# A transformer block's down projection in block products joined to the feed-forward, and the low parts of early weights made by other engines

## The chip, the cores and the metric

The kernel runs on one core of one Trainium2 chip. The metric is device time in microseconds, from launch to end. Engines are called PE (TensorE), DVE (VectorE), ACT (ScalarE), POOL (GpSimd) and SP (SyncE), as in the profile. The program has one launch; nothing is computed on the host apart from laying the inputs out.

## The reference, cut

One block on x of 512 tokens by 1024 channels, float32. All weights are float32.

```
h = rms_norm(x, norm1_pre)
q, k, v, z, xbc, dt, gates = split(h @ w_in)          # 512, 128, 128, 1024, 1536, 32, 2048 columns
attn = gqa_attention(rope(rms_norm(q)), rope(rms_norm(k)), v) @ w_attn_proj     # 8 query, 2 key heads of 64
ssd  = ssd_branch(z, silu(conv5(xbc)), dt, ...) @ w_ssd_proj                    # Mamba-2, both directions
g_attn, g_ssd = split(sigmoid(gates))
x  = x + rms_norm((g_attn * attn + g_ssd * ssd) @ w_out, norm1_post)
h2 = rms_norm(x, norm2_pre)
gate, up = split(h2 @ w_gate_up)                       # 2 x 2816 columns
x  = x + rms_norm((silu(gate) * up) @ w_down, norm2_post)                       # w_down: 2816 x 1024
```

## The kernel before

Every large product is made in a rounded float32 form (fp32r): each operand is split into a high part (a cast, on ACT) and a low part (operand minus high part), and a product is three matmuls, low x high, high x low and high x high. A weight tile is 128 rows by 1024 columns (512 KB). Its low part is made in one of three ways, chosen by a letter in `weights` and read in `wnext`/`presplit`: "v", a subtraction on DVE; "g", a subtraction on POOL; "d", ACT writes the negated weight, rounded to fp32r, into the low part's tile (`A.mul(l, raw, -1.0)`), and an accumulating transfer that POOL issues (`G.dma_start(l, src, accum_op=ALU.add)`) adds the weight from memory, which leaves what the rounding dropped. High and low parts have four buffers each, raw tiles three.

The stages, in order of time in the trace: q projection with the first norm (to 33 us); k/v projection, 8 k-tiles with 12 matmuls each (to 47); `xbc`, the x/B/C projection, 12 weight tiles of 24 matmuls, with convolution, rotary embedding and head norms of q and k woven in (to 131); the z projection woven with attention (to 225); gates woven with the state-space part (to about 375); their projections and the mixing (to 446); `out_proj`; the feed-forward's gate and up projection, 22 tiles of hidden channels (about 492 to 728); the down projection, 22 k-tiles (725 to 846); the last norm and the stores.

In `xbc` the order on PE, ACT, DVE and POOL is the written one (`manual_schedule`), by a table `inner` of what stands in the middle and at the end of each tile: `kt(h)` are the transposes of half of the rotated keys (`k_transposed`, two banks "sb", each read by two copies into `kT`), `xt` those of x. In the feed-forward PE's order is the written one and a scheduler places the other engines' instructions, in which `issue_after` sets a bound. Elsewhere the scheduler decides.

The feed-forward multiplies its first three tiles plainly (`NPLAIN`, `prepare_plain`, `plainly`) and the other 19 by seven block products in place of eight (two halves of tokens, two of channels, gate and up), which need sums R1 to R4 of quarters of h2T; `combine` makes these sums for tokens 256 on, and `blocks2` and `blocks3` bring h2T's last tokens (`hilo`: ACT's high, DVE's low part). `row_rstd` makes a diagonal matrix of the row scales, which PE spreads over the partitions (`spread`). `activate` makes the activation tiles `act`, 22 of 128 hidden channels by 512 tokens.

`down` multiplies plainly: for each k-tile the four groups of 128 tokens by two halves of 512 columns, three matmuls each, 24 matmuls of 512 columns, into eight banks; the last four k-tiles are run token group by token group (`token_major8` with `ntail` 4), so that the epilogue of a group (square sum on ACT, gains and residual on DVE, store) runs beside the matmuls of the next.

## Time and profile before

| | us |
|---|---|
| three runs | 847.55, 851.00, 851.08 (median 851.0) |
| profiled execution | 855.7 |
| its span, first to last instruction | 853.8 |
| PE busy | 822.2 (96%) |
| DVE, ACT, POOL busy | 550.2, 434.2, 178.7 |
| mean granted clock of TensorE | 0.986 of 2.4 GHz |

PE is the engine with the most work, so a step costs time where PE waits for it, where it adds matmuls, or where it stands behind the last matmul. A wait has a second effect in this trace, that the granted clock is lower for some microseconds behind it; the windows show it.

### The profile page before, as it was taken

What the parts mean: (1) busy time and instruction counts of PE and PEld (TensorE: products, weight loads), DVE (VectorE), ACT (ScalarE), POOL (GpSimd) and SP (SyncE); (2) the same over time, 40 slices, a digit from 0 to 9 for tenths busy, and PEclk for the clock granted to TensorE, in tenths of its full rate; (3) what the DMA queues carried; (4) which work ended last, traced back from release to release, by engine and by line L of the source; (5) the groups of instructions that cost most, each with busy time, mean ns of one, the idle gap of its engine ahead of it and who ended that gap; (6) DMA issues with size and microseconds to landing.
All of it is one profiled execution on the core that took longest, in us unless ns stands there. A gap on an engine that the chain in (4) does not pass through costs nothing.

```text
span 853.8 us, 12071 instructions
## 1 busy us (share of the span) xinstructions
PE 822.2 (96%) x4570; PEld 689.6 (81%) x4570; DVE 550.2 (64%) x918; ACT 434.2 (51%) x775; POOL 178.7 (21%) x142
## 2 busy tenths in 40 slices
PE   8989899899899999999999989999999999999996
PEld 7768787666666777767888788999999999888885
DVE  3958884965325545676683796788788788533326
ACT  6656585554664434157333655555555556322222
POOL 3323122310113334539551011000000100000000
PEclk9989999999999999999999999999999999999999
DMA  9586551110676665137335542677666674522314
GB/s 309 173 210 146 118 142 51 50 50 0 149 175 145 162 147 137 62 111 221 124 124 196 174 124 72 183 190 196 187 186 175 174 182 151 182 94 95 99 50 148
DMA packets 42826, 120.88 MB, mean 142 GB/s; under 512 B 5264, under 2 KB 5648, under 8 KB 42768
## 3 DMA queue, kind: packets, MB, share of 16 engines
q1 hardware_dynamic: 36000, 95.46, 32.7%
q0 software_dynamic: 6768, 24.64, 16.9%
q8 instruction: 36, 0.59, 0.3%
q14 instruction: 22, 0.18, 0.1%
HBM read 111.70 MB, written 8.39 MB: 141 GB/s over the span
## 4 chain that ended last, share of the span: by engine, by line
PE 78%; DVE 9%; DMA 4%; issue 4%; ACT 3%; POOL 2%; SPq 0%; DVEq 0%; POOLq 0%; ACTq 0%
PE sa L973 10%; PE mm L177 8%; PE mm L178 8%; PE mm L179 8%; PE sc L973 6%; PE mm L973 3%; PE sb L973 3%; PE sc L177 3%; PE sc L179 3%; PE sc L178 3%; PE sa L178 2%; PE sa L179 2%; PE sa L177 2%; PE sc L678 2%; PE sb L177 2%
## 5 line engine op out<-in xcount | busy, mean ns | idle before, releaser
L142 ACT CAST whi<-raw 128x1024 fp32r<-128x1024 f32 (+3 forms) x85 | 85.0, 1003 | 56.1 <-PE sc L179 49.3
L147 POOL TENSOR_TENSOR wlo<-raw,whi 128x1024 fp32r<-128x1024 f32 (+3 forms) x31 | 65.1, 2105 | 93.5 <-ACT whi L142 91.3
L177 PE MATMUL mm<-hT,wlo 128*128 128x512 f32 x176 | 74.7, 425 | 6.5 <-DMA wlo<-in_w_xbc 4.1
L179 PE MATMUL mm<-hT,whi 128*128 128x512 f32 x176 | 70.3, 400 | 0.0
L178 PE MATMUL mm<-hT,whi 128*128 128x512 f32 x176 | 69.9, 397 | 0.0
L147 DVE TENSOR_TENSOR wlo<-raw,whi 128x1024 fp32r<-128x1024 f32 (+1 forms) x26 | 31.7, 1218 | 53.3 <-ACT whi L142 53.3
L1016 POOL DMA_DIRECT2D raw<-in_w_gu x19 | 16.4, 864 | 219.0 <-DVE wlo L1022 60.6
L1021 ACT CAST whi<-raw 128x512 fp32r<-128x512 f32 (+1 forms) x57 | 41.6, 762 | 36.3 <-PE mm L973 15.5
L1022 DVE TENSOR_TENSOR wlo<-raw,whi 128x512 fp32r<-128x512 f32 (+1 forms) x57 | 47.7, 866 | 18.5 <-ACT whi L1021 18.4
L973 PE MATMUL sa<-R,whi 128*128 128x256 f32 x304 | 56.4, 283 | 0.0
L177 PEld LDWEIGHTS mm<-hT,wlo 128*128 128x128 f32 x176 | 33.8, 192 | 17.0 <-ACT wlo L144 4.7
L973 PEld LDWEIGHTS sa<-R,whi 128*128 128x128 f32 x304 | 47.4, 192 | 0.0
L973 PE MATMUL sa<-R,wlo 128*128 128x256 f32 x152 | 43.0, 283 | 0.0
L144 ACT ACTIVATE wlo<-raw 128x1024 fp32r<-128x1024 f32 x28 | 29.7, 1060 | 25.2 <-PE mm L177 24.3
L178 PEld LDWEIGHTS mm<-hT,whi 128*128 128x128 f32 x176 | 33.8, 192 | 8.9 <-issue 2.4
L179 PEld LDWEIGHTS mm<-hT,whi 128*128 128x128 f32 x176 | 33.7, 192 | 7.8 <-issue 0.5
L145 POOL DMA_DIRECT2D wlo<-in_w_g x16 | 14.0, 872 | 108.2 <-ACT wlo L144 58.4
L639 DVE TENSOR_REDUCE nmax<-sa 128x1 f32<-128x512 f32 x32 | 21.6, 686 | 16.2 <-PE sa L637 15.9
L973 PE MATMUL sa<-h2T,b 128*128 128x256 f32 x228 | 30.5, 283 | 0.0
L1124 DVE TENSOR_TENSOR acl<-act,ach 128x512 fp32r<-128x512 f32 x22 | 14.9, 688 | 23.3 <-ACT ach L1123 23.3
L973 PEld LDWEIGHTS sa<-R,wlo 128*128 128x128 f32 x152 | 29.2, 192 | 0.1
L973 PEld LDWEIGHTS sa<-h2T,b 128*128 128x128 f32 x228 | 28.7, 192 | 0.0
(439 smaller groups left out, 2476.5 us busy)
## 6 DMA issues: line engine op xcount, KB each, us to landing
raw<-in_w_gu SPq DMA_DIRECT2D x44, 512.0 KB, 4.6
raw<-in_w_dn SPq DMA_DIRECT2D x22, 512.0 KB, 3.5
raw<-in_w_gu POOLq DMA_DIRECT2D x19, 512.0 KB, 5.3
raw<-in_w_g SPq DMA_DIRECT2D x16, 512.0 KB, 6.0
wlo<-in_w_g POOLq DMA_DIRECT2D x16, 512.0 KB, 6.7
raw<-in_w_xbc SPq DMA_DIRECT2D x12, 512.0 KB, 4.2
wlo<-in_w_xbc POOLq DMA_DIRECT2D x12, 512.0 KB, 8.0
b<-in_w_gu SPq DMA_DIRECT2D x19, 256.0 KB, 5.5
```

The lines of the kernel that those rows point to most:

```text
L142: self.A.copy(h[:, :n], raw[:, :n])
L144: self.A.mul(l[:, :n], raw[:, :n], -1.0)
L147: e.tensor_tensor(l[:, :n], raw[:, :n], h[:, :n].bitcast(F32), ALU.subtract)
L177: self.T.matmul(o, ll, rh, start=first, stop=False)
L178: self.T.matmul(o, lh, rl, start=False, stop=False)
L179: self.last_mm = self.T.matmul(o, lh, rh, start=False, stop=last)
L639: V.tensor_reduce(nmax, ps, AX.X, ALU.max, negate=True)
L678: self.T.matmul(po[i * HD : i * HD + HD, :], self.vt[:, k, g * HD : g * HD + HD], pts[h - 1 + i][k], start=k == 0, stop=k == NT - 1)
L973: self.T.matmul(dst, x, y[:, k], start=start and k == 0 and i == 0, stop=k == 3 and i == 2, skip_group_check=True)
L1016: G.dma_start(p13, wgu[:, 1:3], accum_op=ALU.add)
L1021: A.copy(dst[0], src)
L1022: lo.tensor_tensor(dst[1], src, dst[0].bitcast(F32), ALU.subtract)
```

## The change

Down projection. The first 6 of the 22 k-tiles stay plain, the first two of these in `down_start`, in which the feed-forward's last open product (`late`, returned by `ffn` as a function) is run behind the first bank. The other 16 k-tiles are taken as two halves of 8 (k), two halves of tokens and two of columns, by seven products of blocks in place of eight. Each product has four stages (`product`, `NG2`): a stage splits one weight pair (`wsplit`, 2 x 512 columns) and two operands (`asplit`, 256 tokens) and multiplies with 12 matmuls of 512 columns; the splits stand one stage ahead of the matmuls in the written order, and the scheduler moves them further ahead as buffers allow. Sums of weight blocks are made in place by accumulating transfers (`chain`, `p3`), sums of activations on DVE (`sums`), sums of results in `sums2`, `second`, `sums6`, `sums3` and `last`. The seventh product runs by token group: 6 matmuls in each stage for group 2, then 24 for group 3. `begin` and `finish` are the two halves of the last norm. Per k-tile the plain form has 24 matmuls, so 16 have 384; the seven products have 7 x 48 = 336.

Elsewhere: the letters of `weights`; one broadcast product in place of four in `row_rstd`; q's head-norm product on POOL; all kT copies on ACT; `kt(1)` half a tile later; `combine` behind the last h2T low part; the third plain tile's weights split by 1024 columns; other pools for some tiles.

```diff
         for k0, kn in ((0, 3), (3, 3), (6, 2)):
-            yield a["w_kv"][:, k0 : k0 + kn, :], kn * 288, "v" if k0 == 0 else "g"
+            yield a["w_kv"][:, k0 : k0 + kn, :], kn * 288, "v" if k0 == 0 else "d"
         for j in range(12):
-            yield a["w_xbc"][j], 1024, "d"
+            yield a["w_xbc"][j], 1024, "g" if j < 3 else "d"
         for n in range(2):
             for i in range(4):
-                yield a["w_z"][n, i], 1024, "g"
+                yield a["w_z"][n, i], 1024, "gd"[n]
...
-        for t in range(NT):
-            V.tensor_scalar(diag[:, t], self.ident, dst[:, t : t + 1], None, ALU.mult)
+        V.tensor_tensor(diag, self.ident.unsqueeze(1).to_broadcast([P, NT, P]), dst.unsqueeze(2).to_broadcast([P, NT, P]), ALU.mult)
...
-        self.V.tensor_tensor(lo, src, hi.bitcast(F32), ALU.subtract)
+        self.last_lo = self.V.tensor_tensor(lo, src, hi.bitcast(F32), ALU.subtract)
...
-        r = self.head_norm(*bb, NQ, self.hr[:, 8 * t : 8 * t + 8])
+        r = self.head_norm(*bb, NQ, self.hr[:, 8 * t : 8 * t + 8], self.G)
...
-                (A.copy if g else V.tensor_copy)(dst, p4[:, :, g])
+                self.A.copy(dst, p4[:, :, g])
...
-        inner = {5: ([], [kt(0)]), 6: ([kt(1)], [xt(0, 0)]), 7: ([xt(0, 1)], [xt(0, 2)]), 8: ([xt(0, 3)], []),
+        inner = {5: ([], [kt(0)]), 6: ([xt(0, 0)], [kt(1)]), 7: ([xt(0, 1)], [xt(0, 2)]), 8: ([xt(0, 3)], []),
...
+            if wide:
+                for i, names in enumerate((("B11", "B12"), ("B22", "B21"))):
+                    hl = [self.wp.tile([P, 1024], F32R, tag=s, name=self.nm(s), bufs=4) for s in ("whi", "wlo")]
+                    A.copy(hl[0], raw[i])
+                    V.tensor_tensor(hl[1], raw[i], hl[0].bitcast(F32), ALU.subtract)
...
-        for t in (2, 3):
-            combine(t)
+        with self.tc.issue_after(self.last_lo.ins):
+            for t in (2, 3):
+                combine(t)
...
-                    w = prepare_plain(j)
+                    w = prepare_plain(j, True)
...
+    def down_start(self, late):
+        self.wseq = ((self.a["w_dn"][j], 1024, "v") for j in range(NF - 2 * PAIRS))
+        self.bank, self.ops = {}, []
+        for k in range(2):
+            self.down_operands(k)
+        for tag, n, ts in (("sc", 0, (2, 3)), ("sb", 0, (0, 1)), ("mm", 1, (0, 1)), ("sa", 1, (2, 3))):
+            for t in ts:
+                self.bank[t, n] = self.ps(tag)
+                for k in range(2):
+                    self.plain(k, t, n)
+                if late:
+                    late = late()
...
+            def prep(g):
+                w = wsplit(b(g))
+                for i in range(2):
+                    kept.append((asplit(a(2 * g + i)), [y[:, i * 512 : i * 512 + 512] for y in w]))
+                if after:
+                    G.dma_start(chain[g], after(g), accum_op=ALU.add)
...
+        def sums6():
+            for t in range(2):
+                c[2 + t, 0] = cs.pop()
+                A.copy(c[2 + t, 0], u[t])
+                add(2 + t, 1, u[t], ALU.subtract)
+                add(t, 1, u[t], ALU.subtract)
+                add(2 + t, 0, x[t])
+                begin(2 + t)
...
+        product(u, lambda g: chain[g], a11, True, lambda g: blk(g, 0, 1),
+                lambda k: V.tensor_tensor(r1[k], a22(k), a21(k), ALU.subtract), then=third_weights)
+        product(v, lambda g: raw(g, 1, 0), a12, False, None, lambda k: V.tensor_tensor(a21(k), a11(k), a21(k), ALU.subtract),
+                then=sums2)
+        product(a, lambda g: chain[g], lambda k: r1[k], True, lambda g: blk(g, 1, 1),
+                lambda k: V.scalar_tensor_tensor(r1[k], r1[k], -1.0, a11(k), ALU.mult, ALU.subtract), then=lambda: second(a))
+        product(x, lambda g: p3[g], a21, True, None,
+                lambda k: V.scalar_tensor_tensor(a12(k), r1[k], -1.0, a12(k), ALU.mult, ALU.subtract), then=lambda: second(x))
+        product(u, lambda g: chain[g], lambda k: r1[k], False, lambda g: blk(g, 1, 0), then=sums6)
+        product(a, lambda g: raw(g, 1, 1), a12, False, then=sums3)
+        product(y, lambda g: chain[g], a22, False, None, lambda k: between.get(k, int)(), lambda: last(2))
+        stages[0][0]()
+        for i, (_, work) in enumerate(stages):
+            if i + 1 < len(stages):
+                stages[i + 1][0]()
+            work()
+        last(3)
```

POOL at the start of the program, from the k/v weights to the fourth x/B/C tile. `wlo` is a weight's low part, `raw` the weight, `whi` its high part; "DMA" is the accumulating transfer. Before:

```order
L147 TENSOR_TENSOR wlo_367<-raw_137,whi_366 128x864
L147 TENSOR_TENSOR wlo_379<-raw_139,whi_378 128x576
L145 DMA wlo_440<-in_w_xbc 128x1024
L145 DMA wlo_447<-in_w_xbc 128x1024
L145 DMA wlo_579<-in_w_xbc 128x1024
L145 DMA wlo_586<-in_w_xbc 128x1024
```

and after:

```order
L147 DMA wlo_364<-in_w_kv 128x864
L147 DMA wlo_377<-in_w_kv 128x576
L149 TENSOR_TENSOR wlo_439<-raw_436,whi_438 128x1024
L149 TENSOR_TENSOR wlo_445<-raw_442,whi_444 128x1024
L149 TENSOR_TENSOR wlo_576<-raw_573,whi_575 128x1024
L147 DMA wlo_582<-in_w_xbc 128x1024
```

The two k/v subtractions and the first three x/B/C transfers have changed places in kind; the fourth tile stays a transfer.

DVE at the start of the feed-forward, between the two parts of h2T's last tokens. `h2T` is the low part of a token group, `R` and `af` are the sums of `combine`, `rv`, `rn`, `ry`, `rt` the steps of the row scale, `diag` the diagonal. Before:

```order
L930 TENSOR_TENSOR R_1073_4535<-af_4174,mm_4419 128x512
L161 TENSOR_SCALAR rv_4517<-rv_4517 128x4
L189 TENSOR_SCALAR rn_4520<-rv_4517 128x4
L932 TENSOR_TENSOR R_1075_4537<-mm_4420,R_1074_4536 128x512
L192 RECIPROCAL ry_4521<-rt_4522 128x4
L933 SCALAR_TENSOR_TENSOR R_1074_4536<-R_1075_4537,af_4174 128x512
L206 TENSOR_TENSOR rt_4522<-ry_4521 128x4
L935 SCALAR_TENSOR_TENSOR af_4176<-R_1074_4536,af_4176 128x512
L207 TENSOR_TENSOR rt_4522<-rt_4522,rn_4520 128x4
L208 SCALAR_TENSOR_TENSOR ry_4521<-rt_4522,ry_4521 128x4
L162 COPY rstd_142<-ry_4521 128x4
L183 TENSOR_TENSOR h2T_3918<-sc_4503,h2T_3916 128x4x128
```

and after:

```order
L208 TENSOR_TENSOR rt_4527<-rt_4527,rn_4525 128x4
L209 SCALAR_TENSOR_TENSOR ry_4526<-rt_4527,ry_4526 128x4
L164 COPY rstd_142<-ry_4526 128x4
L166 TENSOR_TENSOR diag_4535<-cst_100,rstd_142 128x512
L184 TENSOR_TENSOR h2T_3918<-sc_4508,h2T_3916 128x4x128
L184 TENSOR_TENSOR h2T_3919<-sc_4509,h2T_3917 128x4x128
L929 TENSOR_TENSOR R_1078_4537<-af_4174,mm_4424 128x512
L994 TENSOR_TENSOR wlo_4684<-raw_4679,whi_4683 128x1024
L931 TENSOR_TENSOR R_1080_4539<-mm_4425,R_1079_4538 128x512
```

The sums stand behind both low parts now, the diagonal ahead of them, and the first wide low part of the third plain tile among the sums.

DVE at the end of the program. `ss`, `rv`, `rn`, `ry` and `rt` are steps of a token group's row scale, `gn` the gain, `x` the residual, `o` (before) and `c` (after) the result, a bank (`mm`, `sc`) holds the last products. Before:

```order
L218 TENSOR_SCALAR ss_8130<-ss_8130 128x1
L1136 TENSOR_TENSOR o_8128<-sc_7309,gn_7299 128x512
L220 TENSOR_SCALAR rv_8136<-ss_8130 128x1
L1136 TENSOR_TENSOR o_8129<-sc_7310,gn_7301 128x512
L189 TENSOR_SCALAR rn_8138<-rv_8136 128x1
L192 RECIPROCAL ry_8139<-rt_8140 128x1
L204 TENSOR_SCALAR rt_8140<-ry_8139,rn_8138 128x1
L208 SCALAR_TENSOR_TENSOR ry_8139<-rt_8140,ry_8139 128x1
L1134 TENSOR_TENSOR ry_8139<-ry_8139,rstd_142 128x1
L1138 SCALAR_TENSOR_TENSOR o_8128<-o_8128,ry_8139,x_1629_8124 128x512
L1138 SCALAR_TENSOR_TENSOR o_8129<-o_8129,ry_8139,x_1630_8125 128x512
```

and after, where four token groups (c_7410 to c_7405 and their second halves) end near each other:

```order
L1264 TENSOR_TENSOR c_7406<-c_7406,gn_7413 128x512
L1270 SCALAR_TENSOR_TENSOR c_7410<-c_7410,ry_8262,x_1693_8233 128x512
L1270 SCALAR_TENSOR_TENSOR c_7408<-c_7408,ry_8262,x_1692_8232 128x512
L1270 SCALAR_TENSOR_TENSOR c_7409<-c_7409,ry_8283,x_1697_8245 128x512
L1270 SCALAR_TENSOR_TENSOR c_7407<-c_7407,ry_8283,x_1696_8244 128x512
L1266 TENSOR_SCALAR rv_8299<-ss_8073 128x1
L1245 TENSOR_TENSOR c_7405<-c_7405,sc_7326 128x512
L190 TENSOR_SCALAR rn_8301<-rv_8299 128x1
L193 RECIPROCAL ry_8302<-rt_8303 128x1
L205 TENSOR_SCALAR rt_8303<-ry_8302,rn_8301 128x1
L209 SCALAR_TENSOR_TENSOR ry_8302<-rt_8303,ry_8302 128x1
L1268 TENSOR_TENSOR ry_8302<-ry_8302,rstd_142 128x1
```

The addition of the last bank (`c_7405<-c_7405,sc_7326`) stands behind the final products of the first two groups.

## Rows read from the trace of the kernel before

**Rows 1.** Page, part 1: busy us, share of the span, instructions of each engine.

```profile
PE 822.2 (96%) x4570; PEld 689.6 (81%) x4570; DVE 550.2 (64%) x918; ACT 434.2 (51%) x775; POOL 178.7 (21%) x142
```

**Rows 2.** Waits of PE: line, what for, us in total, times, longest.

```profile
PE mm L177 <- DMA wlo<-in_w_xbc: 4.1, 2, 3.6
PE sb L654 <- ACT pt L656: 3.2, 1, 3.2
PE sb L372 <- ACT kT L447: 2.7, 1, 2.7
...
PE sa L178 <- DVE h2T L183: 1.9, 1, 1.9
PE sa L177 <- DVE pl L994: 1.5, 1, 1.5
...
PE sa L286 <- DVE diag L165: 1.3, 1, 1.3
```

**Rows 3.** Windows: stretch, length, busy PE, PEld, DVE, ACT, POOL, clock, DMA share, GB/s.

```profile
57.00:63.00 6.00, 6.00 (x16) 4.59 (x16) 4.81 (x14) 0.00 (x0) 2.98 (x5) 0.53 1.06 279
93.00:99.00 6.00, 5.99 (x27) 5.03 (x28) 4.86 (x8) 3.98 (x7) 0.88 (x1) 0.72 0.19 44
165.00:175.00 10.00, 6.91 (x25) 3.02 (x26) 4.48 (x8) 2.86 (x5) 4.42 (x2) 0.83 0.45 157
510.00:514.00 4.00, 4.00 (x24) 4.00 (x23) 3.92 (x7) 1.73 (x3) 1.20 (x1) 0.59 0.00 0
733.24:744.12 10.88, 10.88 (x50) 9.01 (x48) 3.79 (x5) 3.15 (x4) 0.00 (x0) 1.00 0.56 192
```

**Rows 4.** Timeline at 28 to 57: start, us, instruction, idle before; POOL, then PE.

```profile
29.32 4.46 POOL L147 TENSOR_TENSOR wlo<-raw,whi 128x864 fp32r<-128x864 f32 x2 [3.60 <-ACT whi L142]
...
47.36 0.87 POOL L145 DMA_DIRECT2D wlo<-in_w_xbc  x1 [6.86 <-ACT wlo L144]
...
38.78 0.29 PE L178 MATMUL sb<-wlo,hT 128*128 128x288 f32 x1
...
56.56 0.76 PE L177 MATMUL mm<-hT,wlo 128*128 128x512 f32 x1 [3.59 <-DMA wlo<-in_w_xbc]
```

**Rows 5.** Timeline at 30, DVE.

```profile
29.94 4.38 DVE L183 TENSOR_TENSOR hT<-h,hT 128x512 fp32r<-128x512 f32 x2
```

**Rows 6.** The tile wlo at 36 to 80: its transfers.

```profile
DMA to landing us min/median/max: 7.7/9.1/11.8
```

**Rows 7.** Timeline at 92, DVE, then ACT.

```profile
92.13 0.75 DVE L447 CAST kT<-sb 128x256 fp32r<-128x256 f32 x2
...
92.58 0.70 ACT L447 CAST kT<-sb 128x256 fp32r<-128x256 f32 x2 [5.56 <-DVE kT L447]
```

**Rows 8.** Timeline at 162, POOL, then DVE.

```profile
162.13 4.95 POOL L147 TENSOR_TENSOR wlo<-raw,whi 128x1024 fp32r<-128x1024 f32 x2 [26.04 <-ACT whi L142]
...
162.43 2.48 DVE L515 CAST stl<-ones 128x128 fp32r<-128x128 f32 x1
```

**Rows 9.** Timeline at 505 to 509, ACT, then DVE.

```profile
505.84 0.59 ACT L182 CAST h2T<-sc 128x512 fp32r<-128x512 f32 x1
...
507.56 1.28 DVE L183 TENSOR_TENSOR h2T<-sc,h2T 128x512 fp32r<-128x512 f32 x2
```

**Rows 10.** Groups by form: count | busy us, mean ns | idle before and its releasers.

```profile
L147 DVE TENSOR_TENSOR wlo<-raw,whi 128x1024 fp32r<-128x1024 f32 x25 | 30.6, 1225 | 53.3 <-ACT whi L142 53.3
...
L1022 DVE TENSOR_TENSOR wlo<-raw,whi 128x1024 fp32r<-128x1024 f32 x19 | 23.2, 1220 | 4.8 <-ACT whi L1021 4.8
...
L1021 ACT CAST whi<-raw 128x1024 fp32r<-128x1024 f32 x19 | 19.9, 1049 | 18.1 <-DMA raw<-in_w_gu 15.2 <-PE sa L973 2.9
...
L1099 DVE TENSOR_TENSOR g<-g,sa 128x256 f32<-128x256 f32 x19 | 7.9, 416 | 1.6 <-PE sa L973 1.1 <-ACT g L1098 0.5
```

**Rows 11.** Timeline of the tail from 846, ACT, then DVE.

```profile
846.62 0.69 ACT L153 ACTIVATE junk<-sc,rstd 128x512 bf16<-128x512 f32 x1 [1.94 <-PE sc L179]
...
849.11 1.41 DVE L1138 SCALAR_TENSOR_TENSOR o<-o,ry,x 128x512 f32<-128x512 f32 x2
```

More of the change, by code (lines that the diff above doesn't have):

```diff
@@ L42 @@
 R_DTB, R_AL, R_D, R_QK, R_END = 0, 32, 64, 80, 336
+PAIRS = 8
 NPLAIN = 3
@@ L1038, in ffn @@
         rb = late = None
+        spare = [self.cp.tile([P, S], F32, tag=tag, name=self.nm("act")) for tag in ("lT", "rT", "vt")]
+        spare += [self.tp.tile([P, S], F32, tag="spill", name=self.nm("act"), bufs=2) for _ in range(2)]
         def activate(j, up, sign, g):
@@ L1109, in ffn @@
             late = (j, w, u, x7, pw, g)
-        finish(*late)
-    def down(self):
-        V, A = self.V, self.A
-        g = self.gain("norm2_post", "e")
-        self.wseq = ((self.a["w_dn"][j], 1024, "v") for j in range(NF))
-        split = {}
-        def lhs(k):
-            for i in range(k // 2 * 2, min(k // 2 * 2 + 4, NF), 2):
-                if i not in split:
-                    split[i] = hi, lo = [self.sp.tile([P, 2, S], F32R, tag="R", name=self.nm(n), bufs=8) for n in ("ach", "acl")]
-                    for e in range(2):
-                        A.copy(hi[:, e], self.act[i + e])
-                        V.tensor_tensor(lo[:, e], self.act[i + e], hi[:, e].bitcast(F32), ALU.subtract)
-            return [h[:, k % 2] for h in split[k // 2 * 2]]
-        def epilogue(t, po):
-            x = [self.slot("e", [512], name="x2") for _ in range(2)]
+        return lambda: finish(*late)
@@ new lines, in mm3f, with plain, down_operands @@
+    def mm3f(self, o, a, b, start=False):
+        for i, (x, y) in enumerate(((a[1], b[0]), (a[0], b[1]), (a[0], b[0]))):
+            self.T.matmul(o, x, y, start=start and i == 0, stop=i == 2, skip_group_check=True)
+    def plain(self, k, t, n):
+        ah, al, (wh, wl) = self.ops[k]
+        tok, c = slice(t * P, t * P + P), slice(n * 512, n * 512 + 512)
+        self.mm3f(self.bank[t, n], (ah[:, tok], al[:, tok]), (wh[:, c], wl[:, c]), k == 0)
+    def down_operands(self, k, pool=None):
+        ah, al = (pool.tile([P, S], F32R, tag="pa", name=self.nm("pa"), bufs=6) if pool else self.slot("a", [S], F32R, "pa")
+                  for _ in range(2))
+        self.hilo(ah, al, self.act[k])
+        self.ops.append((ah, al, self.wnext()))
@@ new lines, in down, with third_weights, sums2 @@
+        u = [self.ps("sa") for _ in range(2)]
+        a = [self.ps("mm") for _ in range(2)]
+        x = [self.ps("sb") for _ in range(2)]
+        v, y = [bank[t, 0] for t in (0, 1)], [bank[t, 0] for t in (2, 3)]
+        def third_weights():
+            for g in range(NG2):
+                self.load(p3[g], blk(g, 0, 1))
+                G.dma_start(p3[g], blk(g, 1, 1), accum_op=ALU.add)
+        def sums2():
+            for t in range(2):
+                c[t, 0] = cs.pop()
+                A.copy(c[t, 0], v[t])
+                add(t, 0, u[t])
@@ new lines, in second, with sums3 @@
+        def second(p):
+            for t in range(2):
+                add(2 + t, 1, p[t], ALU.subtract)
+        def sums6():
+            for t in range(2):
+                c[2 + t, 0] = cs.pop()
[4 more added lines that the diff above has]
+                begin(2 + t)
+        def sums3():
+            for t in range(2):
+                add(t, 1, a[t], ALU.subtract)
```

138 lines of the change are left out of this document (112 added, 26 removed).

## The prediction

> **What bounds the kernel now.** I read the busy line of the page first: TensorE is busy 822.2 us of a span of 853.8 [rows 1], so 31.6 us are idle and the rest is matmuls. Then the waits of PE by cause [rows 2], to see at which places the idle time lies. Then the granted clock in windows behind each of these waits [rows 3], because a wait here is followed by matmuls at the lower of the two levels (1.2 instead of 2.4 GHz; a figure of 0.5 is the lower one): a stretch of T us at a mean clock of c loses T x (1 - c). Last the other engines' timelines at these places [rows 4 to 9], to see what ended late and why. The down projection shows no wait of PE at all: 48 matmuls in 10.88 us at a clock of 1.00 [rows 3], 0.2267 us each. It is bound by the number of matmuls; DVE works 3.79 and ACT 3.15 us of that window.
>
> The sum is made against the profiled execution, 855.7 us with a span of 853.8. It lies 4.7 above the median of 851.0, which I take off at the end.
>
> **Part 1, low parts of the early weights.** (a) x/B/C: PE waits for the low part of tile j = 1 3.6 us (4.1 with the 0.5 for j = 0) [rows 2]. POOL issues that transfer at 47.36 [rows 4]; such transfers took 7.7 to 11.8 us to land there [rows 6]. Behind the wait the clock is 0.53 over 6 us [rows 3], a loss of 6 x 0.47 = 2.8. In all 6.9 us. The change lets POOL subtract for j = 0, 1 and 2: 4.95 us for two of that size [rows 8], so 2.4 to 2.5 each; even if the operand of j = 1 were ready only when POOL issued before (47.4), the low part stands at 49.9, against a need at 53.0 (the matmul at 56.56 less its wait [rows 4]) less the 1 us that PE comes earlier. The wait has no successor that I can see for j = 1 and 2. For j = 3, the first by transfer, the buffer and cast are there some 10.9 us (two tiles of 24 matmuls) before PE wants it, against a landing of 9.1 in the middle and 11.8 at most: 0 to 1 us of wait. I take **-6.5** (bounds -3.5 and -6.9).
>
> The price of POOL's subtractions is paid by DVE. The rows show it: a DVE copy of 128 columns took 2.48 us beside POOL's pair at 162 [rows 8], the two h low parts 4.38 us beside POOL at 29.3 [rows 5, 4], against 1.28 for two of the same size at 507.56 [rows 9]. The Trainium skill (SBUF — State Buffer, section "SBUF: two separate sides") states that GpSimd and VectorE, when VectorE has two SBUF inputs, lock a shared port pair for a whole instruction, so that the later of the two stands still; the trace agrees with its 2.48 and 4.38, and by this rule each added instruction of POOL can stop one of DVE's for its whole length, which would make the time that of R2 below. At 47 to 57 it is a transfer that PE waits for and not DVE, so the sum has nothing for this, and R2 has its price.
>
> (b) k/v: the low parts of groups 2 and 3 go from POOL to transfers. DVE's h low parts then need 1.3 instead of 4.38 us [rows 5], and the diagonal, for which PE waits 1.3 [rows 2], is one instruction of 512 columns (0.64 by the pair in 1.28 [rows 9]) instead of four. Against it: ACT's cast of group 2 is done at 29.3, when POOL starts [rows 4]; in the new order two h casts (0.59 each [rows 9]) and a negation (0.9 of the 1.05 for 1024 columns [rows 10]) follow before the transfer, so it is issued at about 31.4 and lands between 39.1 and 43.2 by the 7.7 to 11.8 [rows 6], while k-tile 3 came at 38.6 [rows 4] and would now come 1 us earlier. From 2.5 gained to 3 lost; I take **-1.0**, next to the 7.7: an estimate, since the bytes of other transfers that are under way there are not known.
>
> (c) z, second half: from POOL to transfers. PE waits 3.2 us for attention's transposed probabilities [rows 2], and the clock is 0.83 over 165 to 175 [rows 3], of which PE works about 7 us: 1.2 lost. POOL's pair (4.95) held up a DVE copy on that path for 2.48 [rows 8]. That goes; but ACT gets four negations of 1.05 [rows 10] in a stage in which it also writes the probabilities. Bounds 0 and -4.4; I take **-2.5**.
>
> **Part 2, kT copies and the second kT transpose.** PE waits 2.7 us [rows 2] for a bank that is read by two kT copies of DVE at 92.13, which stand behind DVE's other work; ACT's copies follow DVE's, and ACT had been idle 5.56 us [rows 7]. The clock behind it is 0.72 over 6 us [rows 3]: 1.7 lost. On ACT the copies can start at once, and the second transpose comes half a tile (12 matmuls, 2.7 us) later. **-4.3.** ACT pays for it: four more copies of about 0.35 [rows 7] and a table load more in this stage, over a few us in which PE may wait for a bank: **+1.0** (0 to 2).
>
> **Part 3, start of the feed-forward.** PE waits 1.9 us for the low part of h2T [rows 2], which starts at 507.56 although its high part was cast at 505.84 [rows 9]; the residual combinations stand ahead of it on DVE. After that the clock is 0.59 over 4 us [rows 3]: 1.6 lost. Then 1.5 us for the plain weights of tile 2 [rows 2], split last. The change puts the low part ahead of the combinations and splits these weights wide and early: 5.0, less about 0.5 for the diagonal that now stands before the low part. **-4.5** (bounds -2 and -5.5: g of tile 0 now stands behind some 10 us of DVE work, and its bank is wanted when tile 2 starts).
>
> **Part 4, the down projection.** *Removed:* 528 matmuls become 144 + 336 = 480; 48 x 0.2267 = **-10.9**. *Added beside PE:* each of the 28 stages splits 1024 weight columns and two operands of 256: 1.225 + 2 x 0.42 = 2.06 us on DVE [rows 10], 1.05 + 2 x 0.35 = 1.75 on ACT [rows 7, 10], below the 2.72 us of its 12 matmuls. On top come operand sums: sixteen of 256 columns before the products and sixteen within the first four. The heaviest, the third, has 4 x 2.06 + 8 x 0.42 + 2 x 0.64 = 12.9 us of DVE against 10.88 of PE. Four buffers of weights let the splits run up to four stages ahead, so the 2.0 us too many are covered by work done ahead. All of it is about 68 us of DVE for 76.2 of PE. *Added on the path:* the last product runs by token, so its first half has stages of 6 matmuls, 1.36 us, against 2.06 of DVE, just after six sums and two gains of the sixth product: **+1.5** (0 to 2.5). The sixteen accumulating transfers have two products (21.8 us) to land, against 11.8 at most [rows 6]: nothing. *The join with the feed-forward:* 22.7 us of DVE work for the splits and sums of six plain tiles stand against 32.6 us of PE (6 x 24 x 0.2267): nothing, +2 if an operand of plain tile 5, which stands last, is late. *The tail:* before, from PE's last matmul to the end of the last two products 846.3 to 850.5, then the store [rows 11]. After, DVE and ACT have four square sums on ACT (3.1), a table load (1.3) and square roots, then twelve small steps, six products and six final products, all in front of or around the last token: ordered, they end at about PE's last matmul + 10 instead of + 4.2, since they begin only 6.8 us before it. The row at hand is the 1.41 for two final products and 0.69 for one square [rows 11]. **+5.0** (2 to 6.5). Together **-4.4** (bounds -8 and 0 without rivals).
>
> **Sum.** -6.5 - 1.0 - 2.5 - 4.3 + 1.0 - 4.5 - 4.4 = -22.2; 855.7 - 22.2 = 833.5 for a profiled execution, less 4.7 = 828.8: **829 us**.
>
> **The rivals.**
> *R1, the down projection brings nothing*: the products are held by DVE at each boundary by 0.7 us (six of them) beyond the above, or the tail eats it. For it: the third product exceeds PE's time. Against: the mean is 68 against 76. 829 + 4.4 + 2 = 835.
> *R2, the early stalls come back*: POOL's subtractions and products hold DVE, the kT copies find the operands late, and the k/v low part lands at 43 with a wait of 4 and the clock's loss behind it. Price: half of parts 1 and 2 (6.5) and the k/v wait with its loss (5): 829 + 11.5 = 840.5. For it: 4.38 us for work of 1.28 [rows 5, 9]. Against: the order leaves half a tile and more between these steps and PE.
> *R3, slower*: DVE in the products falls back. If its steps take a tenth longer than in [rows 10], a product with sums exceeds PE by 3 us and the four stages' lead is used up; PE then waits at each boundary, and a wait of 1.9 us was followed by a loss of 1.6 [rows 2, 3], one of 3.6 by 2.8. Six boundaries of 3.5 to 6.4 us are 21 to 38: 850 to 867. It decides from about 22 us of stalls, that is 3.7 at each boundary. For it: DVE's queue is in order and a late split delays those behind. Against: DVE's splits in the feed-forward, beside POOL's transfers, took 1.220 where those elsewhere took 1.225 [rows 10], so the transfers don't lengthen them.
> *R4, it goes better*: the tail costs 2 and the k/v stage gains 2.5, z 4.4: 829 - 3 - 1.5 - 1.9 - 3 = about 819.5.
> *R5, it does not do what it says*: the low parts of x/B/C are late from POOL too, since the raw tile or ACT's cast is what comes late. Then 6.5 stay: 835.5. Against: at 47.36 POOL had waited for ACT's negation, which stands behind that cast [rows 4].
>
> **How the numbers follow.** Forecast 0.52, R1 0.11, R2 0.12, R3 0.09, R4 0.10, R5 0.06. The forecast's own range by its bounds is 822 to 837. Leaving out R3 and the upper half of R2's spread, the range is 818 to 843. A measurement here can tell about 0.5% from no change: faster means under 846.7, slower over 855.3. Faster: forecast, R1, R4, R5 and most of R2 and a little of R3: 0.86; same: 0.07, the lower half of R3 and R2's tail; slower 0.07.
>
> **What would show it.** In the changed profile: no wait for an x/B/C low part at about 52 and a clock of 1.00 from 56 to 63; no wait over 1 us before the kT transposes; DVE copies of 128 columns at 0.28 near 160; the low part of h2T within 0.7 us of its high part and tile 2 starting without a wait; in the products a mean of 10.9 us for four stages with PE waiting under 3 us in all; from the last matmul to the end about 12 us instead of 7.5. It would be wrong if PE waits for a weight or operand split in several products, if the k/v weights land after 41, or if a new wait over 2 us stands in the x/B/C or attention stage.

## The result, and the profile after

The changed kernel took 828.93 us in the median of four runs (826.76 to 830.12) against 850.99 before: a ratio of 0.9747, 95% interval 0.9714 to 0.978, 22.1 us less. The forecast was 829 (818 to 843). The profiled execution of the changed kernel took 830.1 us with a span of 828.2, that of before 855.7 with 853.8, so the two traces differ by 25.6 us. The 3.5 us between the two differences is explained below: the profiled execution of before was one of the longer ones.

The page's busy line of the changed kernel, beside [rows 1]:

```profile
PE 804.9 (97%) x4522; PEld 676.8 (82%) x4522; DVE 578.4 (70%) x999; ACT 465.8 (56%) x841; POOL 200.0 (24%) x162
```

PE works 17.3 us less, of which 48 matmuls account for 10.9; most of the rest is time that matmuls took at the lower clock before. The waits of PE in the changed kernel (line, what for, us in total, times, longest), beside [rows 2]:

```profile
PE sb L179 <- DMA wlo<-in_w_kv: 3.3, 1, 3.3
PE mm L178 <- DMA wlo<-in_w_g: 2.1, 1, 2.1
PE mm L179 <- DMA wlo<-in_w_z: 1.8, 2, 1.3
...
PE sa L179 <- DVE h2T L184: 0.3, 1, 0.3
...
PE sc L1125 <- DVE as L1202: 0.2, 1, 0.2
```

The waits for x/B/C's low part (4.1), for kT (2.7), for the transposed probabilities (3.2), for the plain weights (1.5) and for the diagonal (1.3) are gone, that for h2T's low part went from 1.9 to 0.3. New are 3.3 us for a k/v transfer and 1.8 for z transfers. In the whole down projection (L1125) one wait of 0.2 is left. The windows (columns as in [rows 3]):

```profile
38.00:44.00 6.00, 5.31 (x29) 5.34 (x29) 3.51 (x6) 5.83 (x10) 1.66 (x1) 0.72 0.51 164
...
56.00:62.00 6.00, 6.00 (x28) 4.95 (x28) 5.69 (x12) 3.73 (x6) 3.50 (x5) 1.00 0.69 150
...
88.00:94.00 6.00, 6.00 (x31) 4.96 (x30) 4.23 (x8) 5.27 (x11) 3.25 (x4) 1.00 0.75 183
165.00:175.00 10.00, 9.45 (x58) 7.62 (x57) 8.11 (x20) 5.88 (x15) 0.00 (x0) 1.00 0.60 148
212.00:218.00 6.00, 4.91 (x15) 3.92 (x16) 2.29 (x6) 2.53 (x6) 0.36 (x1) 0.72 1.05 291
490.00:496.00 6.00, 5.42 (x44) 4.99 (x44) 4.33 (x8) 3.97 (x6) 0.16 (x1) 1.00 0.52 87
...
709.04:817.60 108.56, 108.24 (x478) 88.90 (x476) 86.59 (x168) 64.44 (x116) 19.27 (x16) 1.00 0.75 185
```

The clock is 1.00 at all four places where [rows 3] show that it had fallen before. It falls at two new ones, behind the k/v wait (38 to 44) and behind the wait for the first gates weight (212 to 218); the kernel before had that second wait too, 2.4 us, and kept its clock behind it:

```profile
227.00:233.00 6.00, 5.09 (x27) 4.16 (x27) 3.55 (x11) 3.80 (x9) 0.27 (x1) 1.00 1.05 296
```

Each of the two falls loses 1.7 us (6 x 0.28). The last row above is the stretch from the end of the feed-forward's last product to the last matmul: PE works 108.2 of 108.6 us, DVE 86.6.

Where the 25.6 us of span went, by the start of certain matmuls in PE's timeline. The forecast's terms stand beside the change of each stretch.

| stretch, by PE's matmuls | before | after | change | forecast |
|---|---|---|---|---|
| start to first x/B/C matmul | 47.28 | 48.10 | +0.8 | -1.0 |
| to first transpose of keys (86.75; 80.77) | 39.47 | 32.67 | -6.8 | -6.5 |
| to first transpose of queries (116.33; 105.89) | 29.58 | 25.12 | -4.5 | -4.3 |
| to first scores (144.43; 133.96) | 28.10 | 28.07 | 0.0 | +1.0 |
| to first gates matmul (227.91; 213.09) | 83.48 | 79.13 | -4.4 | -2.5 |
| to the feed-forward (492.35; 478.76) | 264.44 | 265.67 | +1.2 | 0 |
| to its fourth tile (534.85; 516.39) | 42.50 | 37.63 | -4.9 | -4.5 |
| to the last matmul (846.14; 817.34) | 311.29 | 300.95 | -10.3 | -10.9 + 1.5 |
| to the end of the span (853.8; 828.2) | 7.66 | 10.86 | +3.2 | +5.0 |

### The profile page after: what moved, and what is told of

It reads as the page before. It is cut to its first block, busy times and chain, and to the rows that moved or that the text cites. A ratio compares the mean times of both kernels' runs of the same rounds, so it can differ in the third digit from the quotient of the medians.

```text
span 828.2 us, 12209 instructions
## 1 busy us (share of the span) xinstructions
PE 804.9 (97%) x4522; PEld 676.8 (82%) x4522; DVE 578.4 (70%) x999; ACT 465.8 (56%) x841; POOL 200.0 (24%) x162
## 4 chain that ended last, share of the span: by engine, by line
PE 83%; DVE 5%; DMA 4%; ACT 3%; issue 2%; POOL 1%; SPq 1%; DVEq 0%; ACTq 0%; POOLq 0%
PE sa L972 10%; PE mm L178 8%; PE mm L179 8%; PE mm L180 8%; PE sc L972 7%; PE sb L1125 4%; PE sa L1125 4%; PE mm L972 3%; PE sb L972 3%; PE mm L1125 3%; PE sc L178 3%; PE sc L180 3%; PE sc L179 3%; PE sc L677 2%; PE sa L179 2%
## 5 line engine op out<-in xcount | busy, mean ns | idle before, releaser
L144 ACT CAST whi<-raw 128x1024 fp32r<-128x1024 f32 (+3 forms) x69 | 68.0, 992 | 20.6 <-PE sc L180 9.8
L149 POOL TENSOR_TENSOR wlo<-raw,whi 128x1024 fp32r<-128x1024 f32 (+1 forms) x28 | 58.2, 2081 | 65.5 <-ACT whi L144 63.9
L146 ACT ACTIVATE wlo<-raw 128x1024 fp32r<-128x1024 f32 (+2 forms) x31 | 32.3, 1043 | 26.4 <-PE mm L178 24.4
L178 PEld LDWEIGHTS mm<-hT,wlo 128*128 128x128 f32 x176 | 33.3, 189 | 11.8 <-issue 3.2
L641 ACT ACTIVATE pr<-sa,nmax 128x512 f32<-128x512 f32 x32 | 22.0, 688 | 14.6 <-DVE rc L643 7.4
L155 ACT ACTIVATE junk<-z 128x512 bf16<-128x512 f32 x8 | 5.0, 628 | 42.6 <-DVE z L785 42.5
```

Of the source, the lines that this page charges most:

```text
L144: self.A.copy(h[:, :n], raw[:, :n])
L146: self.A.mul(l[:, :n], raw[:, :n], -1.0)
L149: e.tensor_tensor(l[:, :n], raw[:, :n], h[:, :n].bitcast(F32), ALU.subtract)
L178: self.T.matmul(o, ll, rh, start=first, stop=False)
L641: self.last_exp = A.activation(pr, ps, AF.Exp, bias=nmax, accum_out=sm)
```

## The experiments

Every run was timed in five rounds beside the kernel before, whose median was 850.2 to 850.3. The interval of a ratio is about 0.25 to 0.45% to either side, 2 to 4 us, so two versions of the changed kernel that differ by 1.5 us in the median are not told apart by time; there the traces decide.

### One half alone: e_early and e_down

`e_early` is the kernel before with all edits ahead of the down projection (but for the pools of some tiles); `e_down` is the changed kernel with these edits taken back, thus the down projection alone:

```diff
-            yield a["w_kv"][:, k0 : k0 + kn, :], kn * 288, "v" if k0 == 0 else "d"
+            yield a["w_kv"][:, k0 : k0 + kn, :], kn * 288, "v" if k0 == 0 else "g"
-            yield a["w_xbc"][j], 1024, "g" if j < 3 else "d"
+            yield a["w_xbc"][j], 1024, "d"
-                yield a["w_z"][n, i], 1024, "gd"[n]
+                yield a["w_z"][n, i], 1024, "g"
...
-                    w = prepare_plain(j, True)
+                    w = prepare_plain(j)
```

> The changed early stages and the feed-forward's start alone; the down projection stays plain with 528 matmuls and its old tail. Theory (each early term is independent of the down projection): the start of the feed-forward's fourth tile lies 18.5 us earlier than before, as in the changed kernel, and nothing behind it moves: about 832.5 us. Rival (the early gain is only there because something in the down projection absorbs it, or is partly clock luck of one execution): 838 or more.

> The down projection in block products alone; low parts, diagonal, head norm, kT copies, combine and plain weights as before. Theory: 48 matmuls less are 10.9 us, of which 10.3 show at the last matmul, and the tail is 3.2 us longer: 7.1 less than before, about 844 us. Rival R1 of the prediction (the block products bring nothing): 851.

Measured: e_early 837.68 us (ratio 0.9848, 0.9814 to 0.9882), 12.5 less than before; e_down 841.20 (0.9897, 0.9864 to 0.993), 9.0 less. The parts add up (21.5 against 22.1): R1 is out. e_down is 2.8 better than its 844, which lies at the edge of its interval. But e_early misses its 832.5 by 5 us and ends within 0.4 of its rival's 838, although its trace has the fourth tile at 516.28, the 18.5 us earlier that were expected, and a span of 835.3. What was wrong is the reference for these 18.5. The trace of e_down, which has the early stages of before, tells why; its waits and windows:

```profile
PE sb L654 <- ACT pt L656: 3.2, 1, 3.2
PE mm L179 <- DMA wlo<-in_w_xbc: 2.7, 1, 2.7
PE sb L374 <- ACT kT L448: 2.7, 1, 2.7
```

```profile
56.00:59.00 3.00, 3.00 (x14) 2.46 (x15) 2.90 (x6) 0.41 (x1) 2.21 (x4) 1.00 1.04 276
...
89.00:92.00 3.00, 2.59 (x16) 2.28 (x17) 1.81 (x4) 3.00 (x7) 0.00 (x0) 1.00 0.16 30
...
162.00:166.00 4.00, 3.03 (x12) 1.92 (x14) 2.34 (x8) 2.31 (x4) 2.06 (x1) 0.65 0.49 163
...
502.00:504.00 2.00, 2.00 (x19) 2.00 (x18) 2.00 (x6) 0.14 (x1) 0.99 (x1) 1.00 0.00 0
```

The same waits as in [rows 2] are there, that for kT as long as before, those for x/B/C and h2T shorter (2.7 and 1.4 against 3.6 and 1.9), but the clock stays at 1.00 behind these three, where [rows 3] show 0.53, 0.72 and 0.59. The fourth tile starts at 526.62 in this execution and at 534.85 in the profiled one of before, from the same early code but for the pools of some tiles. So the loss of clock, 7.3 us of my price list (2.8 + 1.7 + 1.2 + 1.6), is not paid in every execution, and the profiled one of before had paid all of it. The times say the same. Of the 33 executions of the kernel before that stand beside the experiments, the eight with a mean granted clock of 0.994 took 845.3 to 849.3 us, the four with 0.986 or less 853.0 to 856.7; the profiled one had 0.986.

### The low parts of x/B/C, of k/v, and the diagonal: u_xbc, u_kv, u_kx, u_dkx

Each is the changed kernel with letters put back: x/B/C (`u_xbc`), k/v (`u_kv`), both (`u_kx`), and both with the diagonal's four instructions (`u_dkx`).

```diff
-            yield a["w_xbc"][j], 1024, "g" if j < 3 else "d"
+            yield a["w_xbc"][j], 1024, "d"
```

> The changed kernel with the first three x/B/C low parts by transfer again. Theory: the wait of 3.6 us at the second tile and the lower clock behind it (2.8) come back: about 835.5 us, with clock 0.5 to 0.6 in the six us behind the wait. Rival (that wait came from POOL's order and the buffers behind the k/v subtractions, which are gone now): under 831 and no wait over 1 us.

> The changed kernel with the k/v low parts of groups 2 and 3 by POOL's subtraction again. Theory: the new wait of 3.3 us for the k/v transfer and the lower clock behind it (0.72 over 6 us, 1.7) go, DVE's h low parts take 4.4 us again and bring back a wait of about 1 us: 825 to 827 us. Rival (POOL's two subtractions push the x/B/C subtractions back or hold DVE so long that as much is lost): 829 or more.

> The changed kernel with both the k/v and the x/B/C low parts made as before. Theory, formed from the runs with one of them undone (827.7 with k/v back, 830.5 with x/B/C back): each of the two edits alone removes the wait at the second x/B/C tile, since POOL's k/v subtractions are what pushes DVE's and ACT's h work, and so the transfer's issue, some 4 us back. With both undone the wait of 2.7 to 3.6 us and the low clock behind it return: 833 to 836 us. Rival (the two edits add up singly, 828.9 + 1.5 - 1.2): 829.

> The changed kernel with the k/v and x/B/C low parts and also the diagonal's four instructions as before. Theory: the diagonal's 2 us are what is missing in the run with only the low parts undone (there the wait at the second x/B/C tile was 1.4 us and the clock stayed at 1.00); with it back the transfer is issued at 47.4 again, the wait is 2.7 to 3.6 and the clock falls behind it: 833 to 836 us. Rival (the length of that wait is the luck of how fast the transfer lands in one execution, and the diagonal shifts PE and POOL alike): 830 to 831.

Measured: 830.47 us (ratio 0.9772, 0.9736 to 0.9807), 827.69 (0.9731, 0.97 to 0.9762), 830.41 (0.977, 0.9725 to 0.9814) and 831.61 (0.9791, 0.9757 to 0.9825). The theory for u_xbc fell: without POOL's x/B/C subtractions there is no wait at the second x/B/C tile either. The timelines show what sets it: DVE's h work and POOL's issue of that tile's transfer, in u_xbc, u_kx and u_dkx in turn (start, us, instruction, idle before):

```profile
26.85 1.44 DVE L294 SCALAR_TENSOR_TENSOR h<-xT,gcol,rbs 128x512 f32<-128x512 f32 x2
...
29.18 1.28 DVE L184 TENSOR_TENSOR hT<-h,hT 128x512 fp32r<-128x512 f32 x2
...
43.47 0.86 POOL L147 DMA_DIRECT2D wlo<-in_w_xbc  x1 [7.08 <-ACT wlo L146]
```

```profile
26.81 3.24 DVE L294 SCALAR_TENSOR_TENSOR h<-xT,gcol,rbs 128x512 f32<-128x512 f32 x2
...
30.93 2.51 DVE L184 TENSOR_TENSOR hT<-h,hT 128x512 fp32r<-128x512 f32 x2
...
46.48 0.86 POOL L147 DMA_DIRECT2D wlo<-in_w_xbc  x1 [6.84 <-ACT wlo L146]
...
54.23 0.47 PE L178 MATMUL mm<-hT,wlo 128*128 128x512 f32 x1 [1.43 <-ACT sq L344]
```

```profile
29.48 4.45 POOL L149 TENSOR_TENSOR wlo<-raw,whi 128x864 fp32r<-128x864 f32 x2 [4.36 <-ACT whi L144]
...
47.52 0.86 POOL L147 DMA_DIRECT2D wlo<-in_w_xbc  x1 [6.84 <-ACT wlo L146]
...
56.83 0.76 PE L179 MATMUL mm<-hT,wlo 128*128 128x512 f32 x1 [3.64 <-DMA wlo<-in_w_xbc]
```

The transfer waits for ACT's negation, ACT's queue for DVE's h, and DVE's h instructions take longer beside POOL's k/v subtractions (3.24 and 2.51 us against 1.44 and 1.28, 3.0 in all) and stand behind the diagonal. Without these subtractions the issue comes at 43.47, with them at 46.48, 3.0 later, with the old diagonal as well at 47.52 (before 47.36 [rows 4]), and the wait goes from none to 1.4 to 3.6. So three edits do one job. They don't make all of the last step: of the 2.2 us between u_kx and u_dkx, 1.0 is the later issue, and 1.6 that the transfer took 9.2 us to land against 7.6, less 0.4 by which PE came later itself. With k/v made by transfer PE waits 2.0 to 3.7 us in the k/v stage instead, by execution (in u_xbc the page puts it down to `ACT q L303`, where the transfer is what came late), which also pushes the need back. u_kv, which has the x/B/C edit alone, has neither wait; its PE waits 2.1 us in three pieces for h's low parts, the clock stays at 1.00 over 38 to 50, and it is the lowest median of all. Against the changed kernel this is 1.2 us, within the interval: not shown to be faster. u_kx, at 830.41, misses its 833 and lies nearer its rival's 829: the wait is back, but at 1.4 us and with a clock of 1.00 behind it. u_dkx stands between its two expectations by time (831.61 against 833 or more and 831 or less). Its trace shows what the theory says, 3.64 us of wait and a clock of 0.72 behind it, but its rival, the luck of the landing, has the larger part in the step from u_kx:

```profile
56.00:62.00 6.00, 5.17 (x17) 4.18 (x18) 5.59 (x15) 0.41 (x1) 3.48 (x5) 0.72 1.05 273
```

### The kT edits and the head norm: u_kt and u_hnkt

```diff
-        inner = {5: ([], [kt(0)]), 6: ([xt(0, 0)], [kt(1)]), ...
+        inner = {5: ([], [kt(0)]), 6: ([kt(1)], [xt(0, 0)]), ...
-                self.A.copy(dst, p4[:, :, g])
+                (self.A.copy if g else self.V.tensor_copy)(dst, p4[:, :, g])
```

and in u_hnkt also q's head-norm product back from POOL to DVE (`self.G` to `self.V`).

> The changed kernel with the kT copies half on DVE again and the second key transpose in the middle of its tile again. Theory: the wait of 2.7 us and the lower clock behind it (1.7) return: about 833 us. Rival (the wait came from DVE being late after the x/B/C stall, which is gone): under 830.5, no wait over 1 us there.

> The changed kernel with the kT copies, the second key transpose and also q's head-norm product as before, on DVE. Theory: that product's four 0.69 on DVE are what kept the wait away in the run with only the kT edits undone; with them back, DVE's queue is late again and the wait of 2.7 us with its clock loss returns: 833 us. Rival (the wait of before hangs on the x/B/C stall ahead of it): 830 to 831 and no wait over 1 us.

Measured: 830.19 us (ratio 0.9755, 0.9711 to 0.9799) and 835.63 (0.982, 0.9793 to 0.9848). With the kT edits alone undone nothing comes back: from 76 to 100 PE works all the time at a clock of 1.00. With the head norm undone too, the wait is larger than before the change, 3.7 against 2.7, with a lower clock behind it than in [rows 3]:

```profile
PE sb L373 <- ACT kT L447: 3.7, 1, 3.7
```

```profile
88.00:94.00 6.00, 5.71 (x20) 4.74 (x21) 4.74 (x9) 4.26 (x8) 0.88 (x1) 0.55 0.25 47
```

The theory of u_hnkt holds and that of u_kt falls: DVE's work on q is what made the kT copies late, and taking four products off DVE is enough. The x/B/C stall ahead of it is not the cause, since the wait returns here without that stall. Whether the kT edits would be enough by themselves was not tried. The pair is worth 6.7 us here and not 4.3: PE's first key transposes come 5.8 us sooner than before (81.00 against 86.75), DVE's kT copies only 4.7 (87.41 against 92.13 [rows 7]), and the clock falls further behind the longer wait.

### z: u_z

```diff
-                yield a["w_z"][n, i], 1024, "gd"[n]
+                yield a["w_z"][n, i], 1024, "g"
```

> The changed kernel with all z low parts by POOL's subtraction again. Theory: the wait of 3.2 us for the transposed probabilities and about 1 us of lower clock return, the 1.8 us of waits for z transfers go: about 831.5 us. Rival (the two cancel): 829.

Measured 832.8 us (ratio 0.9792, 0.9746 to 0.9838). PE's wait for the probabilities is back as it was, and those for z transfers are gone. The lower clock that the theory added is not there in this execution, the window right behind the wait has 1.00:

```profile
PE sb L653 <- ACT pt L655: 3.2, 1, 3.2
```

```profile
158.00:162.00 4.00, 4.00 (x21) 1.78 (x22) 1.28 (x3) 1.38 (x2) 2.36 (x1) 1.00 0.37 122
```

From the first scores to the gates it is 81.9 us (134.24 to 216.16) against 79.1, 2.8 more. The theory holds for the waits, and the median is 3.9 above the changed kernel, where 2.5 were forecast.

### The feed-forward's start: u_ffn

```diff
-        with self.tc.issue_after(self.last_lo.ins):
-            for t in (2, 3):
-                combine(t)
+        for t in (2, 3):
+            combine(t)
-                    w = prepare_plain(j, True)
+                    w = prepare_plain(j)
```

> The changed kernel with combine where it was and the third plain tile's weights split by 512 columns again. Theory: waits of 1.4 to 1.9 us for h2T's low part and 1.5 us for the weights return with 1.6 us of lower clock: 833 to 834 us, the fourth tile starting 4.9 us later. Rival (the feed-forward gives the time back later, at its first block products): 829 to 830.

Measured 832.86 us (ratio 0.9797, 0.9754 to 0.984), 3.9 more than the changed kernel. Both waits are back, but the clock stays at 1.00 behind them (windows 494 to 496 and 507 to 511); the stretch to the fourth tile takes 40.4 us (477.78 to 518.17) against 37.6 and 42.5:

```profile
493.22 0.39 PE L179 MATMUL sa<-h2T,ph 128*128 128x256 f32 x1 [1.39 <-DVE h2T L184]
...
507.19 0.47 PE L178 MATMUL sa<-h2T,pl 128*128 128x512 f32 x1 [1.47 <-DVE pl L1001]
...
806.68 0.50 PE L1124 MATMUL mm<-wlo,as 128*128 128x512 f32 x1 [1.37 <-DVE wlo L1195]
```

The theory holds for the two waits (2.8 us). The trace has 2.1 us more of waits in the down projection, 1.4 in the sixth block product and 0.7 in the last, where the changed kernel has 0.2 (and it lacks that kernel's fall of the clock behind the gates wait, 1.7). That side effect was not expected; that the scheduler placed the splits otherwise would explain it and was not looked into.

One sum over the undone edits: u_dkx, u_hnkt, u_z and u_ffn, which between them undo every early edit, lose 2.7 + 6.7 + 3.9 + 3.9 = 17.2 us, while all early edits together gained 12.5 in e_early. What an edit loses when it is undone is not what it gains when it is put in: the kT wait came back a microsecond longer than it had been, and u_ffn made waits elsewhere. The sum is of medians that are each good to 2 to 4 us.

### How much room DVE has in the products: x_dve

```diff
-            V.tensor_tensor(t[:, 1], src, t[:, 0].bitcast(F32), ALU.subtract)
+            for _ in range(2):
+                V.tensor_tensor(t[:, 1], src, t[:, 0].bitcast(F32), ALU.subtract)
```

> The changed kernel with the low part of each block-product operand computed twice on DVE, two more instructions of 256 columns for each of 28 stages: DVE's work in the products goes from about 68 to 87 us against 76 of PE. Theory (the splits run ahead and PE is held only by the sum): PE's waits are many and short, 10 to 14 us in all: 840 to 843 us, clock at 1.00. R3 of the prediction (a late DVE makes a few long waits at the product boundaries with a lower clock behind each): 850 us or more. If the products had much more room than counted: under 834.

Measured 841.92 us (ratio 0.9898, 0.9873 to 0.9923), 13.0 more. DVE's busy time from the feed-forward's last product to the last matmul rises from 86.6 to 105.1 us and the stretch from 108.3 to 120.2 (709.47 to 829.68). The sum is the theory's (840 to 843), the shape is more like R3's, a long wait with a lower clock behind it:

```profile
789.56 0.47 PE L1125 MATMUL sa<-whi,as 128*128 128x512 f32 x1 [1.37 <-DVE as L1203]
806.61 0.77 PE L1125 MATMUL mm<-whi,as 128*128 128x512 f32 x1 [5.89 <-DVE as L1203]
```

```profile
806.00:812.00 6.00, 5.39 (x15) 4.28 (x16) 6.00 (x14) 0.69 (x2) 0.00 (x0) 0.58 0.01 3
```

Four waits make 8.8 us, one of them 5.9 in the sixth product (from 797.84), a stage behind its start, where DVE had made the sums of the fifth and had itself stood 2.1 us for a square sum of ACT. The lower clock followed. Of 18.5 us of added DVE work 8.8 reach PE as waits, and about 3 more as the lower clock, so the changed kernel left DVE some 6.5 us of room if the clock is counted and some 9.7 if it is not: an estimate, since it hangs on where the work is added. R3's condition (DVE's steps a tenth longer, some 7 to 9 us) would by this estimate have used up most of that room, and cost little beyond it.

### A shorter tail: b1

The changed kernel with k/v by POOL, and with the finished half of token groups 0 and 1 squared and multiplied by its gain in the fifth product:

```diff
+        def early(t):
+            half[t] = new("es", [16], 2)[:, :2]
+            self.square_sum(half[t][:, 1:2], c[t, 0], self.rstd[:, t : t + 1])
+            V.tensor_tensor(c[t, 0], c[t, 0], gain[0], ALU.mult)
...
-        product(u, lambda g: chain[g], lambda k: r1[k], False, lambda g: blk(g, 1, 0), then=sums6)
+        product(u, lambda g: chain[g], lambda k: r1[k], False, lambda g: blk(g, 1, 0),
+                lambda k: {2: lambda: early(0), 5: lambda: early(1)}.get(k, int)(), then=sums6)
```

> The changed kernel with k/v low parts by POOL again and with the square sums and gain products of the first two token groups' finished half moved from the end into the fifth product, two DVE products and two ACT squares fewer near the end. Theory (DVE and ACT are behind at the end): from PE's last matmul to the end 8.5 to 9.5 us instead of 10.9, 826 us. Rival (the last group's own chain of sum, square, root, products and store sets the tail): 10.5 or more, 827.7 as with k/v alone.

Measured 828.15 us (ratio 0.9737, 0.9709 to 0.9764): nothing against u_kv. From the last matmul to the end it is 10.0 us (815.50 to 825.5) instead of 10.8 in u_kv (813.86 to 824.7), but the stretch ahead of it takes 109.8 us (705.73 to 815.50) instead of 108.1, with these waits:

```profile
PE mm L1125 <- DVE wlo L1196: 0.7, 1, 0.7
PE sc L1125 <- DVE as L1202: 0.7, 2, 0.5
```

Both theory and rival missed: the tail is shorter by 0.8 and not by 1.4 to 2.4, and the same DVE and ACT work set earlier meets the room of the products, which x_dve shows to be small in the sixth. In the tail itself, DVE no longer holds the last group's sum back (it waits 0.29 for PE), and what is left is that group's chain behind group 2's:

```profile
815.93 0.69 DVE L1245 TENSOR_TENSOR c<-c,sc 128x512 f32<-128x512 f32 x1 [0.29 <-PE sc L1125]
...
820.79 1.42 DVE L1276 SCALAR_TENSOR_TENSOR c<-c,ry,x 128x512 f32<-128x512 f32 x2
```

## Why the prediction was right, and where its steps were not

The number is right to 0.1 us in the median, which is partly luck: see the clock below. Five of the nine stretches are within one us of their terms; the other four are off by 1.2 to 1.9 us, two up and two down, and all nine together by 3.4. Step by step:

- *Down projection, matmuls.* Right. 48 less are 10.9 us, and the stretch gained 10.3; e_down alone gained 9.0 in the median, with the tail in it.
- *The last product's +1.5.* Too high: one wait of 0.2. The splits run far enough ahead that the half-length stages find them done. In e_down and u_ffn, with the same down projection, the waits of the sixth and last products are 1.0 and 2.1, so the margin is small.
- *The tail's +5.0.* Too high, 3.2. I let the square sums begin 6.8 us before PE's last matmul; ACT began them 9.5 us before it, at 807.89, since DVE made the sums of the sixth product (807.11) ahead of the last operand splits (808.30 and 810.10). DVE was then behind by one us only, at the last group's sum:

```profile
807.89 0.72 ACT L155 ACTIVATE junk<-c,rstd 128x512 bf16<-128x512 f32 x1 [0.76 <-DVE c L1245]
...
815.85 2.73 DVE L1270 SCALAR_TENSOR_TENSOR c<-c,ry,x 128x512 f32<-128x512 f32 x4
818.50 0.21 DVE L1266 TENSOR_SCALAR rv<-ss 128x1 f32<-128x1 f32 x1
818.62 0.68 DVE L1245 TENSOR_TENSOR c<-c,sc 128x512 f32<-128x512 f32 x1
...
823.48 1.41 DVE L1270 SCALAR_TENSOR_TENSOR c<-c,ry,x 128x512 f32<-128x512 f32 x2
```

- *x/B/C, -6.5.* The size is that of the profiled execution (6.8), the cause was only one of three. I gave it to POOL's x/B/C subtractions; beside the new diagonal they suffice (u_kv), but u_xbc has no such wait without them. The k/v letter, the x/B/C letter and the diagonal each shorten it, and with all three undone (u_dkx) it is 3.6 again. As the median goes, the three together are 2.7 us, inside the interval.
- *k/v, -1.0.* Wrong in sign: +0.8. Up to the first k/v matmul PE gained 2.6 us (32.97 to 30.35). Not all of it is the diagonal and the h low parts: before, the clock had also fallen at 8 to 12 us,

```profile
8.00:12.00 4.00, 4.00 (x12) 3.10 (x11) 0.97 (x2) 2.96 (x7) 2.34 (x2) 0.57 0.97 333
```

and e_early, which has the edits and that fall, has the matmul at 31.65, so they gained 1.3. The k/v transfer cost 3.3 us of wait and 6 us at a clock of 0.72, 1.7. I set the landing at the lower end of the range; the two transfers took 8.7 and 9.0:

```profile
wlo<-in_w_kv POOLq DMA_DIRECT2D x1, 432.0 KB, 8.7
wlo<-in_w_kv POOLq DMA_DIRECT2D x1, 288.0 KB, 9.0
```

They were issued at 29.8 and 30.9, the first earlier than I had it, but PE came 2.6 us earlier too, where I had 1. The landing sets the end of the wait: in e_early it comes at 38.59 and here at 38.55, and PE, later in e_early, waits 2.0 there. The bounds (2.5 gained to 3 lost) held for the stretch.
- *kT, -4.3.* The size is that of the profiled execution (4.5), the step is half wrong: u_kt shows that the moved copies and the moved transpose are not needed for it, u_hnkt that the head norm's place decides. I had counted that edit only as a risk to DVE (R2).
- *ACT's +1.0.* Nothing of it is seen (0.0).
- *z, -2.5.* Too small, 4.4 in the trace and 3.9 by u_z. The lower clock behind the wait was 10 x 0.17 = 1.7 us and not the 1.2 I took, since PE worked through all of it, and ACT's negations cost PE nothing that shows apart from 1.8 us of waits for transfers.
- *The feed-forward's start, -4.5.* Right, 4.9; u_ffn gives 3.9 back. The low part of h2T follows its high part at once (492.40 after 491.78), the diagonal ahead of it having been done at 490.8, so that the 0.5 for it was not paid either, and g of tile 0 held nothing up.
- *Gates to the feed-forward, nothing.* The +1.2 there is the fall of the clock behind the gates wait. The four traces with that fall (changed kernel, e_early, u_hnkt, x_dve) take 264.8 to 265.7 us for this stretch, the ten without it, before among them, 263.4 to 264.4.
- *The clock.* I priced it as a fixed part of each wait. e_down, u_z and u_ffn show the same or similar waits without it. That this did not spoil the number is luck in part: I took the difference from the profiled execution to the median, 4.7 us, off at the end, which happens to be about what the profiled execution of before had paid beyond others. The sum against its own time was 3.4 us too small (22.2 against 25.6); the profiled execution of the changed kernel is only 1.2 above its median, and the two errors of 3.4 and 3.5 cancel.
- *The rivals.* R1 is out by e_down. R2 happened in one part, the k/v wait, at the price it had there (about 5). R3 did not happen, and x_dve puts its point at some 6.5 to 10 us of further DVE work. R4 went half its way (tail, z); the last 3 us of its sum name no term. R5 is out: the wait is gone. The forecast's bounds, added up, give 819 to 846 and not the 822 to 837 that stand as its own range.

On POOL and DVE the trace after bears out the forecast's rows. Three of DVE's h products take 2.06 us alone and 4.21 beside POOL's first x/B/C subtraction (the row of POOL):

```profile
29.83 2.06 DVE L294 SCALAR_TENSOR_TENSOR h<-xT,gcol,rbs 128x512 f32<-128x512 f32 x3
...
33.62 4.21 DVE L294 SCALAR_TENSOR_TENSOR h<-xT,gcol,rbs 128x512 f32<-128x512 f32 x3
...
33.58 2.38 POOL L149 TENSOR_TENSOR wlo<-raw,whi 128x1024 fp32r<-128x1024 f32 x1 [1.82 <-ACT whi L144]
```

The Trainium skill (SBUF — State Buffer, section "SBUF: two separate sides") states that a GpSimd instruction that reads SBUF and a VectorE instruction with two SBUF inputs exclude each other for a whole instruction. The trace agrees with its 2.06 and 4.21. The 2.48 of [rows 8], which the forecast counted as an instance of it, is a copy with one input; with POOL's z subtraction gone that copy takes 0.28 (at 151.07).

What stays open: whether u_kv is better than the changed kernel by its 1.2 us, whether the kT edits do anything that the head norm's place does not, how much of the x/B/C wait is the diagonal's, and what decides in one execution that the clock stays.
